# Sums and stores of the down products' left sides moved behind the next pair's weights; residual rows fetched one at a time

## The chip, the cores and the metric

One core of a Trainium2 chip runs the kernel. The metric is device time in microseconds (us) of one execution; lower is better.

## The reference

One transformer-like block on 1024 tokens (and 16 meta tokens) of width 1024. A Mamba-2 branch and a differential-attention branch are merged into `h`; the change touches only what follows, the feed-forward part:

```python
u2 = rmsnorm(h, norm_ffn_g)
h = h + (silu(u2 @ w_gate_ffn) * (u2 @ w_up_ffn)) @ w_down_ffn
out = rmsnorm(h, norm_final_g)
```

`w_gate_ffn` and `w_up_ffn` are 1024 x 2816, `w_down_ffn` is 2816 x 1024, all float32.

## The kernel before

Every float32 product is made of three matmuls of split operands: a side is rounded (`hi`, by ACT's CAST) and the rest kept (`lo`, a subtraction on POOL or DVE, both in `split_to`, L919 and L920). The three feed-forward products are cut by Strassen's scheme: seven half-size products replace eight, and the sides of the products are sums of quarters.

The hidden columns are worked in 11 pairs of 128-row blocks (`pair` 0 to 10). A pair has a gate half and an up half. Each half loads its weights in two parts (`Weights.load`, L948): the first, "kh0", goes into one of two buffers of the tag `raw`; the second, "kh1", into the tag `ht`, whose five buffers hold four tiles of product 7's right side for the whole loop, so that all kh1 parts share one buffer. `Weights.make` builds seven sides from them (L986 on DVE, then the split; sides 3 and 4 are split straight from the loaded tile). `Half.run` makes the seven products in the order 2, 5, 4, 3, 1, 6, 7 (L1000, 12 matmuls each, 168 a pair), and DVE folds them into the tile `gu` (L1015 to L1026). Product 3 starts on its bank when L1017 has read it, product 7 when L1022 has. In the text 2g is product 2 of the gate half, 3u product 3 of the up half.

`up_out` (L1045 to L1048) multiplies silu(gate) by up. `left_sides` then makes the left sides of the down products on DVE (L1058, L1061, L1063, L1064, L1065; L1026 and L1048 must come first for the last three) and stores them to DRAM (`hid_d`): three stores of 256 KB and one of 1 MB (L1067).

The down products run as 77 steps `s` (7 products of 11 steps, 48 matmuls in 4 banks by three, 12 a step). A step loads a left side (`ra`, 256 KB) and one or two quarters of `w_down_ffn` (`rb`, 256 KB each), five steps deep, and splits them on ACT and DVE (`down_make`). Steps 0 to 4 are loaded in the last pair; from step 5 on the pool `dn` is used, which also holds the eight residual rows blocks `hr0` to `hr7` (512 KB each) and `gf` (512 KB). `add_part` adds finished banks to the rows.

All loads and stores go through SP's queue in order. The order of the instructions on each engine is made from the written program by a scheduler that models time, so a moved line can move its neighbours too; each engine then executes in that order.

Of the kernel before, what the change touches and what calls it, by code (L numbers as in the profile page):

```python
# [9 lines left out]
F32 = mybir.dt.float32  # L10
F32R = mybir.dt.float32r
AF = mybir.ActivationFunctionType
ALU = mybir.AluOpType
# [4 lines left out]
P = 128  # L18
D = 1024
# [4 lines left out]
NT = SEQ // P  # L24
# [18 lines left out]
def tile_hybrid_block(  # L43
# [7 lines left out]
    nc = tc.nc  # L51
# [9 lines left out]
    def nm(s):  # L61
        seq[0] += 1
        return f"{s}_{seq[0]}"
# [69 lines left out]
    h_d = dram([SEQ, D], "h_d")  # L133
    hid_d = dram([7, FF // 2, 512], "hid_d")
# [113 lines left out]
    def gates_block(b):  # L248
# [9 lines left out]
        out=gbh, in0=par[:, PR_GB : PR_GB + 16], scalar1=0.5, scalar2=None, op0=ALU.mult  # L258
# [3 lines left out]
        out=g08, in0=par[:, PR_SUB : PR_SUB + 1], scalar1=1.0 - LAM_INIT, scalar2=None,  # L262
# [4 lines left out]
    with tc.tile_pool(name="ssd", bufs=1, reuse_waits="tile") as sp:  # L267
# [4 lines left out]
        def t2(name, tag="t2", bufs=4):  # L272
# [6 lines left out]
            out=tri, in_=tri, pattern=[[1, P]], compare_op=ALU.is_ge, fill=0.0, base=0,  # L279
# [5 lines left out]
            out=sel, in_=sel, pattern=[[0, P]], compare_op=ALU.is_ge, fill=0.0, base=-(P - 1),  # L285
# [7 lines left out]
            out=cbh, in0=par[:, PR_CB : PR_CB + 12], scalar1=0.5, scalar2=None, op0=ALU.mult  # L293
# [19 lines left out]
            out=wd[:, :, 2 * H : 3 * H], in0=wdr, in1=wd[:, :, 0:H].bitcast(F32), op=ALU.subtract  # L313
# [4 lines left out]
            out=fold, in0=ident[: 4 * H, 0:H], in1=ident[: 4 * H, 2 * H : 3 * H], op=ALU.add  # L318
# [89 lines left out]
        for b in (8, 9, 10, 11, 0, 1, 2, 3, 4, 5, 6, 7):  # L408
            if b == 0:
# [10 lines left out]
                out=hh[:, :L], in0=raw[:, 0:L], scalar1=cwh[:, b, 0:1], scalar2=cbh[:, b : b + 1],  # L420
                op0=ALU.mult, op1=ALU.add,
            )
            for k in range(1, 4):
                nc.vector.scalar_tensor_tensor(
                    out=hh[:, :L], in0=raw[:, k : k + L], scalar=cwh[:, b, k : k + 1],
                    in1=hh[:, :L], op0=ALU.mult, op1=ALU.add,
# [6 lines left out]
            else:  # L433
                act = cT[:, b - 10, :]
            nc.vector.scalar_tensor_tensor(
                out=act, in0=raw[:, :L], scalar=1.0, in1=hh[:, :L], op0=ALU.add, op1=ALU.mult
# [19 lines left out]
        for c in range(NC):  # L456
# [8 lines left out]
            for g in range(2):  # L465
# [4 lines left out]
                if last:  # L470
# [3 lines left out]
                    out=v8(xds[:R]), in0=v8(xdt[:R]), in1=bc(dst, g), op=ALU.mult  # L474
# [8 lines left out]
                else:  # L483
                    nc.gpsimd.tensor_tensor(
                        out=v8(snew), in0=v8(prev[g]), in1=bc(cdk, g), op=ALU.mult
# [6 lines left out]
            for g in range(2):  # L492
# [7 lines left out]
                out=cbm, in0=pcb[:, : 2 * P].rearrange("p (g l) -> p g l", g=2),  # L500
                in1=tri.unsqueeze(1).to_broadcast([P, 2, P]), op=ALU.mult,
            )
            y = t4("y")
            for g in range(2):
# [7 lines left out]
                for hq in range(2):  # L512
# [3 lines left out]
                    for j in range(4):  # L516
                        nc.vector.tensor_scalar(
                            out=m3[:, j, :], in0=b3[:, hq * 4 + j, :],
# [5 lines left out]
                        out=m3, in0=m3, in1=cbm[:, g, :].unsqueeze(1).to_broadcast([P, 4, P]),  # L524
                        op=ALU.mult,
# [13 lines left out]
                    out=v8(xD), in0=v8(xs[:, c, gs]),  # L539
                    in1=dsk[:, g * 8 : g * 8 + 8].unsqueeze(2).to_broadcast([P, 8, HD]),  # L540
                    op=ALU.mult,
# [11 lines left out]
    with tc.tile_pool(name="att", bufs=1, reuse_waits="tile") as ap:  # L553
# [6 lines left out]
            out=base, in_=base, pattern=[[-1, L]], compare_op=ALU.is_ge, fill=-1e30,  # L560
# [3 lines left out]
        for i, a in enumerate((lambda_q1, lambda_q2, lambda_k1, lambda_k2)):  # L564
# [7 lines left out]
            out=lam[:, 2:3], in0=lam[:, 1:2], in1=lam[:, 0:1], op=ALU.subtract  # L572
# [3 lines left out]
            out=nlam, in0=lam[:, 2:3], scalar1=-LAM_INIT, scalar2=None, op0=ALU.add  # L576
# [5 lines left out]
        for t in vms + ams:  # L582
            nc.vector.tensor_scalar(
                out=t, in0=base[:, : t.shape[1]], scalar1=0.0, scalar2=None, op0=ALU.mult
# [3 lines left out]
        for i in range(2):  # L588
            for c in range(2):
                z = slice(64 - 64 * c, 128 - 64 * c)  # L590
                nc.gpsimd.tensor_scalar(
                    out=kls[i][c][z], in0=base[z], scalar1=0.0, scalar2=None, op0=ALU.mult
# [7 lines left out]
        for h in range(AH):  # L600
# [21 lines left out]
            def evac_k(ps, o, w):  # L622
# [22 lines left out]
                out=vm[64 : 64 + NM], in0=ptm[:NM, :P], in1=vm[:NM].bitcast(F32),  # L645
                op=ALU.subtract,
            )
            for q in range(2):
                pt = ps_mm()
                for j in range(4):  # L650
# [6 lines left out]
                    out=vl[:, sl4, :], in0=p3, in1=vh[:, sl4, :].bitcast(F32), op=ALU.subtract  # L657
# [6 lines left out]
            for pr2 in range(NT // 2):  # L664
                arows = []
                for i in (2 * pr2, 2 * pr2 + 1):
# [9 lines left out]
                    for comp, (qt, kt) in enumerate(((q0, k0), (q1, k1))):  # L676
                        S = ap.tile([P, L], F32, tag="S", name=nm("S"), bufs=6)
                        sts.append(S)
                        for n, (o, w) in enumerate(pieces):
# [10 lines left out]
                                out=S[:, o : o + w], in0=ps[:, :w],  # L690
                                in1=base[:, L - W + o : L - W + o + w], scale=1.0,
# [5 lines left out]
                            out=nmx, in0=mx[:, col : col + 1], scalar1=-slope, scalar2=None,  # L697
# [11 lines left out]
                        out=rho, in0=sm[:, 0:1], scalar=nlam, in1=sm[:, 3:4], op0=ALU.mult,  # L709
# [195 lines left out]
    fp = ffn_pool.__enter__()  # L905
# [30 lines left out]
    class Weights:  # L936


        def __init__(self, w, pair):
            self.w, self.pair, self.m, self.two_ = w, pair, {}, {}  # L940
            self.load()
# [90 lines left out]
    def gate_banks():  # L1032
        return ps_mm(), ps_mm(), ps_sc(), ps_sc()
# [18 lines left out]

    SLOT = {1: 0, 2: 1, 5: 2, 6: 3, 3: 4, 4: 5, 7: 6}

    def left_sides(G, U, pair):
        rows = slice(pair * P, (pair + 1) * P)
        a11, a12, a21, a22 = G[:, 0, T1], G[:, 1, T1], G[:, 0, T2], G[:, 1, T2]
        vtt(out=U[:, 0, T2], in0=a21, in1=a22, op=ALU.add)  # L1058
        nc.sync.dma_start(hid_d[SLOT[4], rows, :], a22)
        d = fp.tile([P, 512], F32, tag="tmp", name=nm("d"), bufs=3)  # L1060
        vtt(out=d, in0=a12, in1=a22, op=ALU.subtract)  # L1061
        nc.sync.dma_start(hid_d[SLOT[7], rows, :], d)
        vtt(out=U[:, 0, T1], in0=a11, in1=a22, op=ALU.add)  # L1063
        vtt(out=U[:, 1, T1], in0=a11, in1=a12, op=ALU.add)  # L1064
        vtt(out=U[:, 1, T2], in0=a21, in1=a11, op=ALU.subtract)  # L1065
        nc.sync.dma_start(hid_d[SLOT[3], rows, :], a11)
        nc.sync.dma_start(  # L1067
            hid_d[0:4, rows, :].rearrange("s p t -> p s t"),
            U.rearrange("p a (b t) -> p (a b) t", t=512),
        )  # L1070

    def w_out_rows(t, before_last=None):
        hts = []
# [165 lines left out]
    up_w.make(7)  # L1239
    up.run(7)  # L1240
    up_out(G, U, up, 0)
    left_sides(G, U, 0)

    NP = NF // 2
    downs = [(i, f) for i in (1, 5, 4, 7, 3, 2, 6) for f in range(NP)]
# [51 lines left out]
    for pair in range(1, NP):  # L1297
        G, U = new_pair()
        last = pair == NP - 1
        for w in (w_gate_ffn, w_up_ffn):  # L1300
            gate_side = w is w_gate_ffn
            A = Weights(w[0], pair)
            A.make(*order7)
            h = Half(A, G if gate_side else U, (gate_banks if gate_side else up_banks)())
            if last and not gate_side:
                for s, pool in ((0, st), (1, wk)):
                    down_load(s, f512(fp, "tmp", 3), f1k(st, "raw", 2))
                    down_make(s, f512(fp, "tmp", 3), *pair_of(pool))
                h.run(*order7[:5])
                down_load(2, f512(fp, "tmp", 3), f1k(st, "raw", 2))  # L1310
                down_make(2, f512(fp, "tmp", 3), *pair_of(st))
                h.run(*order7[5:])
                for s in (3, 4):
                    down_load(s, f512(st, "gt", 2), f1k(st, "raw", 2))
            else:
                h.run(*order7)
            if gate_side:
                gate_out(G, h)
            else:
                up_out(G, U, h, pair)  # L1320
                left_sides(G, U, pair)

    b4 = gate_banks()
    for s in range(3):
        down_mm(downs, b4, [(s, j) for j in range(4)])
# [4 lines left out]
    with tc.tile_pool(name="dn", bufs=1, side="right", reuse_waits="tile") as dn:  # L1330
# [7 lines left out]
        def dn_load(s):  # L1338
            if s < len(downs) and s > 4:
                down_load(s, f512(dn, "ra", 5), f1k(dn, "rb", 5))  # L1340
# [2 lines left out]
        dn_make(4)  # L1343
        rows = []
        for r in range(NT):
            ht = dn.tile([P, D], F32, name=f"hr{r}")
            nc.sync.dma_start(ht, h_d[r * P : (r + 1) * P, :])
            rows.append(ht)
        gf = dn.tile([P, D], F32, name="gf")
        nc.sync.dma_start(gf, norm_final_g.partition_broadcast(P))  # L1350
        for s in range(5, 9):
            dn_load(s)
        parts = {
            1: ((0, 0, 1), (1, 1, 1)), 2: ((1, 0, 1), (1, 1, -1)), 3: ((0, 1, 1), (1, 1, 1)),
            4: ((0, 0, 1), (1, 0, 1)), 5: ((0, 0, -1), (0, 1, 1)), 6: ((1, 1, 1),),
# [28 lines left out]
        def store(r, n):  # L1384
            nc.sync.dma_start(out2[r * P : (r + 1) * P, N2[n]], jks[r][:, N2[n]])
# [17 lines left out]
        for p in range(7):  # L1403
            i = downs[p * NP][0]
            banks = b4 if p == 0 else (up_banks if p % 2 else gate_banks)()
            for f in range(3 if p == 0 else 0, NP):
                s = p * NP + f
                dn_load(s + 4)
                if s + 2 < len(downs) and s + 2 > 4:
                    dn_make(s + 2)  # L1410
                if p < 6 or f < NP - 2:
                    down_mm(downs, banks, [(s, j) for j in range(4)])
                elif f == NP - 1:
                    down_mm(downs, banks, [(q, j) for j in range(4) for q in (s - 1, s)])
                for _ in range(2 if i in (2, 6) else 1):
                    if later:
                        later.pop(0)()
            for t, n, sign in parts[i]:
                for j in range(4):
                    if p < 6:  # L1420
                        later.append(
                            lambda a=(i, banks[j], j, t, n, sign): add_part(*a)
                        )
            if i == 3:
                later += [lambda r=r: first_rows(r) for r in range(4)]
            if i == 2:
                for j in range(4):
                    later.append(lambda r=4 + j: (square(r, 0), gain(r, 0, nc.gpsimd)))
# [62 lines left out]
```

## Time and profile before

| what | value |
|---|---|
| median of 3 runs | 2026.34 us (2026.12 to 2028.18) |
| the profiled execution | 2029.1 us |
| its span, first to last instruction | 2026.7 us |
| matmuls on TensorE (PE) busy | 1923.2 us, 95% of the span |
| VectorE (DVE) busy | 1252.8 us, 62% |
| GpSimd (POOL) busy | 567.1 us, 28% |
| DMA moved | 241.38 MB |

PE's busy time counts overlapping matmuls, so 95% is not the share of its peak. What counts is when PE sits idle and at which of its two clock levels it runs.

### The profile page before, as it was taken

The numbers are of one execution on the slowest core, as the hardware profiler recorded it, in microseconds if no ns is written. First come the engines' busy times: TensorE is split into PE (matmuls) and PEld (weight loads), VectorE is DVE, ScalarE is ACT, GpSimd is POOL, SyncE is SP. The second block draws the span as 40 slices with busy tenths as digits, with TensorE's granted clock in tenths as the row PEclk, the third lists the DMA queues.
The fourth block names the chain that finished last, engine by engine and source line by source line (L and its number), as shares of the span: only waits on it lengthen the run. The fifth ranks groups of instructions, "written<-read, shape, count | busy, mean of one in ns | idle before, by whom it ended". The sixth has DMA issues, their size and how long they took to land.

```text
span 2026.7 us, 27727 instructions
## 1 busy us (share of the span) xinstructions
PE 1923.2 (95%) x10478; PEld 1668.0 (82%) x10478; DVE 1252.8 (62%) x2387; ACT 762.1 (38%) x1443; POOL 567.1 (28%) x363
## 2 busy tenths in 40 slices
PE   7999999999999999999999999889999998969998
PEld 7999777789999999888978899767777776758886
DVE  5656678555766566654663443585566656648887
ACT  5333222245555455553331124532222222224454
POOL 2223444411111111110122244344444544400002
PEclk9999999999999999999999999999999999989999
DMA  5111344311111211123765444322322232368865
GB/s 174 49 33 53 97 140 133 112 45 50 53 45 46 61 51 40 51 68 121 253 226 173 151 156 160 111 89 84 93 78 92 80 113 85 114 250 304 313 218 198
DMA packets 185935, 241.38 MB, mean 119 GB/s; under 512 B 13517, under 2 KB 128442, under 8 KB 185802
## 3 DMA queue, kind: packets, MB, share of 16 engines
q1 hardware_dynamic: 185658, 239.09, 36.7%
q8 instruction: 82, 1.34, 0.3%
q10 hardware_dynamic: 144, 0.52, 0.1%
q14 instruction: 51, 0.42, 0.1%
HBM read 181.48 MB, written 53.84 MB: 116 GB/s over the span
## 4 chain that ended last, share of the span: by engine, by line
PE 77%; DVE 13%; DMA 6%; issue 1%; ACT 1%; POOL 0%; SPq 0%; DVEq 0%; POOLq 0%; ACTq 0%
PE mm L108 14%; PE mm L109 14%; PE mm L110 14%; PE sc L1000 5%; PE tp L1000 4%; DVE sm L986 3%; DMA raw<-in_w_up_ffn_dram 3%; PE mm L1000 3%; PE sc L109 2%; PE sc L108 2%; PE sc L110 2%; PE tp L729 2%; PE sc L681 1%; PE sc L684 1%; PE sc L529 1%
## 5 line engine op out<-in xcount | busy, mean ns | idle before, releaser
L89 POOL TENSOR_TENSOR wlo<-raw,whi 128x1024 fp32r<-128x1024 f32 x68 | 176.4, 2594 | 685.8 <-ACT whi L87 614.3
L108 PE MATMUL mm<-uTh,whi 128*128 128x346 f32 (+2 forms) x1008 | 360.4, 358 | 7.5 <-DVE kl L626 2.4
L109 PE MATMUL mm<-uTh,wlo 128*128 128x346 f32 (+2 forms) x1008 | 359.5, 357 | 0.0
L110 PE MATMUL mm<-uTl,whi 128*128 128x346 f32 (+2 forms) x1008 | 358.8, 356 | 0.0
L108 PEld LDWEIGHTS mm<-uTh,whi 128*128 128x128 f32 x1008 | 190.9, 189 | 28.5 <-issue 8.4
L110 PEld LDWEIGHTS mm<-uTl,whi 128*128 128x128 f32 x1008 | 191.0, 189 | 18.7 <-issue 3.9
L109 PEld LDWEIGHTS mm<-uTh,wlo 128*128 128x128 f32 x1008 | 190.9, 189 | 17.7 <-issue 3.4
L920 POOL TENSOR_TENSOR wlo<-sm,whi 128x512 fp32r<-128x512 f32 x88 | 129.7, 1493 | 161.9 <-ACT whi L919 161.9
L919 ACT CAST whi<-sm 128x512 fp32r<-128x512 f32 x88 | 52.7, 619 | 215.4 <-DVE sm L986 95.8
L700 ACT ACTIVATE S<-S,mx 128x272 f32<-128x272 f32 (+7 forms) x128 | 101.0, 791 | 54.7 <-DVE mx L696 53.1
L986 DVE TENSOR_TENSOR sm<-raw,raw 128x512 f32<-128x512 f32 x66 | 54.6, 864 | 67.8 <-DMA raw<-in_w_up_ffn_dram 64.5
L920 POOL TENSOR_TENSOR lo<-raw,hi 128x512 fp32r<-128x512 f32 x44 | 65.5, 1488 | 88.8 <-ACT hi L919 88.8
L87 ACT CAST whi<-raw 128x1024 fp32r<-128x1024 f32 x68 | 71.2, 1047 | 50.6 <-PE mm L110 41.9
L748 DVE TENSOR_TENSOR atl<-tp,ath 128x512 fp32r<-128x512 f32 (+1 forms) x80 | 50.5, 634 | 61.8 <-ACT ath L747 61.5
L986 DVE TENSOR_TENSOR sm<-raw 128x512 f32<-128x512 f32 x44 | 50.6, 1154 | 58.7 <-DMA raw<-in_w_gate_ffn_dram 37.7
L1000 PE MATMUL mm<-t2a,hi 128*128 128x512 f32 x176 | 65.8, 433 | 21.8 <-DVE gu L1017 17.7
L919 ACT CAST dhi<-ra 128x512 fp32r<-128x512 f32 x72 | 44.7, 621 | 109.8 <-issue 53.6
L689 DVE CUSTOM_DVE_ANT_0 S<-sc,base 128x272 f32<-128x272 f32 (+7 forms) x128 | 62.0, 493 | 28.2 <-PE sc L684 27.0
L681 PE MATMUL sc<-k,q 128*128 128x144 f32 (+6 forms) x224 | 76.7, 349 | 1.7 <-ACT S L700 1.1
L689 DVE CUSTOM_DVE_ANT_0 S<-sc,base,mx 128x348 f32<-128x348 f32 (+4 forms) x96 | 56.1, 585 | 34.6 <-PE sc L684 31.2
L108 PE MATMUL mm<-whi,uTh 128*128 128x256 f32 x256 | 73.9, 290 | 3.5 <-ACT whi L100 3.3
L109 PE MATMUL mm<-whi,uTl 128*128 128x256 f32 x256 | 74.8, 293 | 0.1
(398 smaller groups left out, 5200.7 us busy)
## 6 DMA issues: line engine op xcount, KB each, us to landing
raw<-in_w_in_dram SPq DMA_DIRECT2D x60, 512.0 KB, 4.0
rb<-in_w_down_ffn_dram SPq DMA_DIRECT2D x82, 256.0 KB, 5.4
ra<-hid_d SPq DMA_DIRECT2D x74, 256.0 KB, 4.6
raw<-in_w_gate_ffn_dram SPq DMA_DIRECT2D x24, 512.0 KB
raw<-in_w_up_ffn_dram SPq DMA_DIRECT2D x24, 512.0 KB, 5.8
hid_d<-gu SPq DMA_DIRECT2D x11, 1024.0 KB, 5.1
rb<-in_w_down_ffn_dram SPq DMA_DIRECT2D x22, 512.0 KB, 6.3
bcs<-acs_d SPq DMA_DIRECT2D x16, 512.0 KB, 5.0
```

Of the source, the lines that this page charges most:

```text
L87: nc.scalar.copy(hi, raw)
L89: nc.gpsimd.tensor_tensor(out=lo, in0=raw, in1=hi.bitcast(F32), op=ALU.subtract)
L108: nc.tensor.matmul(ps, lh, rh, start=first, stop=False)
L109: nc.tensor.matmul(ps, ll, rh, start=False, stop=False)
L110: nc.tensor.matmul(ps, lh, rl, start=False, stop=last)
L681: nc.tensor.matmul(ps[:, :w], qt[:, qs], kt[:, o : o + w], start=True, stop=False)
L689: nc.vector.tensor_tensor_reduce(out=S[:, o : o + w], in0=ps[:, :w], in1=base[:, L - W + o : L - W + o + w], scale=1.0, scalar=-3e38 if n ...
L700: nc.scalar.activation(S[:, :W], S[:, :W], AF.Exp, scale=slope, bias=nmx, accum_out=sm[:, comp : comp + 1],)
L919: nc.scalar.copy(hi, src)
L920: eng.tensor_tensor(out=lo, in0=src, in1=hi.bitcast(F32), op=ALU.subtract)
L986: vtt(out=tmp, in0=a, in1=b, op=op)
L1000: nc.tensor.matmul(ps, a[:, ki, :], b, start=first and ki == 0 and n == 0, stop=ki == KH - 1 and n == 2, skip_group_check=True,)
```

## The change

`left_sides` becomes a class with two methods. `sums()` makes the same five DVE operations, now written behind the next pair's gate `make`. `store()` issues the same four stores, now written behind the load of the next pair's up weights. After the last pair both follow at once, as before. In the down products the rows and `gf` are no longer fetched ahead of the loads of steps 5 to 8: one row follows the loads at steps 5, 7, 9 and one at each step from 11 on, `gf` comes at step 33. And `dn_load(s + 4)` is called only for `s > 4`; before, it was also called at steps 3 and 4, which loaded steps 7 and 8 a second time.

```diff
-    def left_sides(G, U, pair):
...
+    class LeftSides:
...
+        def sums(self):
+            G, U = self.G, self.U
...
+            self.d = fp.tile([P, 512], F32, tag="tmp", name=nm("d"), bufs=3)
+            vtt(out=U[:, 0, T2], in0=a21, in1=a22, op=ALU.add)
+            vtt(out=self.d, in0=a12, in1=a22, op=ALU.subtract)
+            vtt(out=U[:, 0, T1], in0=a11, in1=a22, op=ALU.add)
+            vtt(out=U[:, 1, T1], in0=a11, in1=a12, op=ALU.add)
+            vtt(out=U[:, 1, T2], in0=a21, in1=a11, op=ALU.subtract)
+
+        def store(self):
+            G, U, rows = self.G, self.U, self.rows
+            nc.sync.dma_start(hid_d[SLOT[7], rows, :], self.d)
+            nc.sync.dma_start(hid_d[SLOT[3], rows, :], G[:, 0, T1])
+            nc.sync.dma_start(hid_d[SLOT[4], rows, :], G[:, 1, T2])
+            nc.sync.dma_start(
+                hid_d[0:4, rows, :].rearrange("s p t -> p s t"),
+                U.rearrange("p a (b t) -> p (a b) t", t=512),
+            )
...
             A = Weights(w[0], pair)
+            if not gate_side:
+                before.store()
             A.make(*order7)
+            if gate_side:
+                before.sums()
...
                 up_out(G, U, h, pair)
-                left_sides(G, U, pair)
-
+                before = LeftSides(G, U, pair)
+
+    before.sums()
+    before.store()
...
-            ht = dn.tile([P, D], F32, name=f"hr{r}")
-            nc.sync.dma_start(ht, h_d[r * P : (r + 1) * P, :])
-            rows.append(ht)
+            rows.append(dn.tile([P, D], F32, name=f"hr{r}"))
         gf = dn.tile([P, D], F32, name="gf")
-        nc.sync.dma_start(gf, norm_final_g.partition_broadcast(P))
         for s in range(5, 9):
             dn_load(s)
+        fetch = [(rows[r], h_d[r * P : (r + 1) * P, :]) for r in range(NT)]
...
-                dn_load(s + 4)
+                if s > 4:
+                    dn_load(s + 4)
+                if s in (5, 7, 9) or s >= NP and fetch:
+                    nc.sync.dma_start(*fetch.pop(0))
+                if s == 3 * NP:
+                    nc.sync.dma_start(gf, norm_final_g.partition_broadcast(P))
```

New line numbers: the sums are L1065 to L1069, the 1 MB store L1076, the other stores L1073 to L1075, the down loads L1259 and L1271, the rows L1424, `gf` L1426.

**SP's queue in the pair loop.** One pair's stretch in the middle of the loop. Of the `raw` loads the first of two from the same tensor is kh0, the second kh1. Before:

```order
L1059 DMA hid_d<-gu_14196 128x512
L1062 DMA hid_d<-d_14473 128x512
L1066 DMA hid_d<-gu_14196 128x512
L1067 DMA hid_d<-gu_14196 128x4x512
L948 DMA raw_14621<-in_w_up_ffn_dram 128x4x256
L948 DMA raw_14767<-in_w_gate_ffn_dram 128x4x256
L948 DMA raw_14769<-in_w_gate_ffn_dram 128x4x256
L948 DMA raw_14904<-in_w_up_ffn_dram 128x4x256
```

Now:

```order
L948 DMA raw_14900<-in_w_up_ffn_dram 128x4x256
L948 DMA raw_14902<-in_w_up_ffn_dram 128x4x256
L1075 DMA hid_d<-gu_14471 128x512
L1073 DMA hid_d<-d_14795 128x512
L1074 DMA hid_d<-gu_14471 128x512
L1076 DMA hid_d<-gu_14471 128x4x512
L948 DMA raw_15042<-in_w_gate_ffn_dram 128x4x256
L948 DMA raw_15044<-in_w_gate_ffn_dram 128x4x256
```

The up kh1 load stood behind the 1 MB store and now stands ahead of all four; the gate kh0 load of the pair after stands behind the 1 MB store. In three of the pairs (every third) that gate load stands two rows higher, ahead of the last two stores.

**DVE in the pair loop**, from the last folds of one pair (`gu_14481`, now `gu_14471`) on; `sm` are the sums of weights. Before:

```order
L1047 TENSOR_TENSOR gu_14481<-gu_14481 128x512
L1058 TENSOR_TENSOR gu_14481<-gu_14481 128x512
L1061 TENSOR_TENSOR d_14758<-gu_14481 128x512
L986 TENSOR_TENSOR sm_14773<-raw_14767,raw_14769 128x512
L986 TENSOR_TENSOR sm_14779<-raw_14767,raw_14769 128x512
L1026 TENSOR_TENSOR gu_14481<-tp_14659,gu_14481 128x512
L1048 TENSOR_TENSOR gu_14481<-gu_14481 128x512
L986 TENSOR_TENSOR sm_14791<-raw_14767,raw_14769 128x512
L1063 TENSOR_TENSOR gu_14481<-gu_14481 128x512
L1064 TENSOR_TENSOR gu_14481<-gu_14481 128x512
L1065 TENSOR_TENSOR gu_14481<-gu_14481 128x512
L986 TENSOR_TENSOR sm_14910<-raw_14904,raw_14906 128x512
```

Now:

```order
L1066 TENSOR_TENSOR d_14795<-gu_14471 128x512
L986 TENSOR_TENSOR sm_14910<-raw_14900,raw_14902 128x512
L986 TENSOR_TENSOR sm_14916<-raw_14900,raw_14902 128x512
L1026 TENSOR_TENSOR gu_14471<-tp_14659,gu_14471 128x512
L986 TENSOR_TENSOR sm_14928<-raw_14900,raw_14902 128x512
L1048 TENSOR_TENSOR gu_14471<-gu_14471 128x512
L1067 TENSOR_TENSOR gu_14471<-gu_14471 128x512
L1068 TENSOR_TENSOR gu_14471<-gu_14471 128x512
L1069 TENSOR_TENSOR gu_14471<-gu_14471 128x512
L1017 TENSOR_TENSOR gu_14756<-mm_14802,gu_14756 128x512
L1019 TENSOR_TENSOR gu_14756<-mm_14801,gu_14756 128x512
L986 TENSOR_TENSOR sm_15072<-raw_15042 128x512
```

The sums of the gate's weights are gone from here (they are made ahead of the folds of the up half), the sums of the up weights (`sm_14910` on) stand ahead of the three left-side sums, and L1017 of the next gate behind these; in two of three pairs L1017 stands higher, ahead of these three sums. The last row reads the gate kh0 load that follows the 1 MB store.

**SP's queue from the last pair to the down products.** Before:

```order
L1067 DMA hid_d<-gu_15336 128x4x512
L1347 DMA hr_15733<-h_d 128x1024
L1347 DMA hr_15735<-h_d 128x1024
L1347 DMA hr_15737<-h_d 128x1024
L1347 DMA hr_15739<-h_d 128x1024
L1347 DMA hr_15741<-h_d 128x1024
L1347 DMA hr_15743<-h_d 128x1024
L1347 DMA hr_15745<-h_d 128x1024
L1347 DMA hr_15747<-h_d 128x1024
L1350 DMA gf<-in_norm_final_g_dram 128x1024
L1250 DMA ra_15751<-hid_d 128x512
```

Now:

```order
L1076 DMA hid_d<-gu_15326 128x4x512
L1259 DMA ra_15742<-hid_d 128x512
L1271 DMA rb_15743<-in_w_down_ffn_dram 128x512 x2
L1259 DMA ra_15747<-hid_d 128x512
L1271 DMA rb_15748<-in_w_down_ffn_dram 128x512 x2
L1259 DMA ra_15752<-hid_d 128x512
L1271 DMA rb_15753<-in_w_down_ffn_dram 128x512 x2
L1259 DMA ra_15757<-hid_d 128x512
L1271 DMA rb_15758<-in_w_down_ffn_dram 128x512 x2
L1259 DMA ra_15802<-hid_d 128x512
L1271 DMA rb_15803<-in_w_down_ffn_dram 128x512 x2
L1424 DMA hr_15733<-h_d 128x1024
```

Nine transfers of 512 KB stood between the store and step 5's loads; now the loads of steps 5 to 9 follow the store, and the first row comes behind them.

## Rows read from the trace of the kernel before

**Rows 1.** Waits of PE, 1400 to 1790 us: us in total, times, longest.

```profile
PE mm L1000 <- DVE gu L1017: 17.7, 9, 2.3
PE tp L1000 <- DVE gu L1022: 6.3, 8, 0.8
PE av L1000 <- ACT whi L919: 5.7, 8, 0.7
```

**Rows 2.** Timeline of PE: start, duration, [idle before, and what ended it].

```profile
1612.74 0.49 PE L1000 MATMUL av<-t2b,whi 128*128 128x512 f32 x1 [0.71 <-ACT whi L919]
...
1632.40 0.50 PE L1000 MATMUL mm<-t2a,hi 128*128 128x512 f32 x1 [1.92 <-DVE gu L1017]
...
1652.60 0.50 PE L1000 MATMUL tp<-b,whi 128*128 128x512 f32 x1 [0.78 <-DVE gu L1022]
...
1656.35 0.50 PE L1000 MATMUL av<-t2b,whi 128*128 128x512 f32 x1 [0.71 <-ACT whi L919]
```

**Rows 3.** Timeline of DVE, the same pair.

```profile
1619.64 1.78 DVE L1065 TENSOR_TENSOR gu<-gu 128x512 f32<-128x512 f32 x1
1628.16 1.90 DVE L986 TENSOR_TENSOR sm<-raw,raw 128x512 f32<-128x512 f32 x3 [6.74 <-DMA raw<-in_w_up_ffn_dram]
...
1631.66 0.68 DVE L1017 TENSOR_TENSOR gu<-mm,gu 128x512 f32<-128x512 f32 x1
...
1647.16 0.86 DVE L986 TENSOR_TENSOR sm<-raw 128x512 f32<-128x512 f32 x1 [2.24 <-DMA raw<-in_w_up_ffn_dram]
```

**Rows 4.** Timeline of SP's queue, the same pair.

```profile
1621.44 0.37 SPq L1067 DMA_DIRECT2D hid_d<-gu  x1
1621.91 0.46 SPq L948 DMA_DIRECT2D raw<-in_w_up_ffn_dram  x1
...
1643.33 0.37 SPq L948 DMA_DIRECT2D raw<-in_w_up_ffn_dram  x1
```

**Rows 5.** Timeline of ACT and POOL, the same pair.

```profile
1613.64 0.61 ACT L919 CAST hi<-raw 128x512 fp32r<-128x512 f32 x1
...
1617.42 1.74 POOL L920 TENSOR_TENSOR lo<-raw,hi 128x512 fp32r<-128x512 f32 x1
```

**Rows 6.** The chain of waits: start, us, what it was.

```profile
1434.12 1.21 DVE sm L986 x2
...
1463.83 5.54 PE sc L1000 x24
...
1744.56 1.20 DVE sm L986 x2
```

**Rows 7.** Timeline of DVE behind the last pair.

```profile
1794.21 0.69 DVE L1063 TENSOR_TENSOR gu<-gu 128x512 f32<-128x512 f32 x1
```

**Rows 8.** Timeline of SP's queue behind the last pair.

```profile
1796.13 0.37 SPq L1067 DMA_DIRECT2D hid_d<-gu  x1
1796.61 5.39 SPq L1347 DMA_DIRECT2D hr<-h_d  x8
...
1805.46 0.32 SPq L1250 DMA_DIRECT2D ra<-hid_d  x1
```

**Rows 9.** Timeline of ACT and PE, step 5.

```profile
1815.13 0.62 ACT L919 CAST dhi<-ra 128x512 fp32r<-128x512 f32 x1 [17.17 <-DMA ra<-hid_d]
...
1818.36 0.80 PE L108 MATMUL mm<-dhi 128*128 128x512 f32 x1 [15.19 <-ACT dhi L919]
```

**Rows 10.** Windows: busy us (instructions) of PE, PEld, DVE, ACT, POOL; PEclk, DMA share, GB/s.

```profile
1498.00:1503.00 5.00, 4.58 (x13) 3.62 (x14) 2.59 (x3) 1.53 (x3) 3.83 (x3) 0.66 0.02 3
...
1815.00:1826.00 11.00, 7.64 (x24) 6.06 (x24) 5.39 (x9) 3.72 (x7) 0.00 (x0) 0.64 1.04 381
1826.00:1836.00 10.00, 9.81 (x44) 7.91 (x43) 9.10 (x15) 6.47 (x12) 0.00 (x0) 1.00 1.04 386
```

**Rows 11.** The page's DMA issues: count, KB each, median us to landing.

```profile
ra<-hid_d SPq DMA_DIRECT2D x74, 256.0 KB, 4.6
hid_d<-gu SPq DMA_DIRECT2D x11, 1024.0 KB, 5.1
```

More of the change, by code (lines that the diff above doesn't have):

```diff
@@ L1053, in tile_hybrid_block, with __init__ @@
     SLOT = {1: 0, 2: 1, 5: 2, 6: 3, 3: 4, 4: 5, 7: 6}
-    def left_sides(G, U, pair):
[L1056 to L1070, printed above, removed]
+    class LeftSides:
+        def __init__(self, G, U, pair):
+            self.G, self.U, self.rows = G, U, slice(pair * P, (pair + 1) * P)
+        def sums(self):
+            G, U = self.G, self.U
+            a11, a12, a21, a22 = G[:, 0, T1], G[:, 1, T1], G[:, 0, T2], G[:, 1, T2]
+            self.d = fp.tile([P, 512], F32, tag="tmp", name=nm("d"), bufs=3)
[13 more added lines that the diff above has]
+            )
     def w_out_rows(t, before_last=None):
@@ L1241, in tile_hybrid_block @@
     up_out(G, U, up, 0)
-    left_sides(G, U, 0)
+    before = LeftSides(G, U, 0)
     NP = NF // 2
```

## Prediction

> **What bounds the kernel now.** PE. I read the waits of PE over the pair loop first: what holds it there are three things, once a pair each [rows 1]. The timeline of PE shows them in one pair: 0.71 us for a cast, 1.92 for L1017, 0.78 for L1022 [rows 2]. The next pair's first product starts 43.61 us after this one's (1612.74 to 1656.35). Undisturbed, 24 matmuls take 5.54 us [rows 6], 0.231 each, so 168 take 38.8. With the three waits that is 42.2. Of the 1.4 that remain I put half to the two matmuls behind the first, which wait for casts as well, and leave half with PE as gaps that stay (my choice; no row parts them). So a pair without waits would take about 39.5 us.
>
> Over seven pairs the mean is (1744.56 - 1434.12) / 7 = 44.35 us [rows 6], 0.74 more than the pair above. Behind some L1017 waits PE runs at the lower level: 13 matmuls in 4.58 us at a granted clock of 0.66, a mixture of 1.2 and 2.4 GHz [rows 10], against 3.0 at 0.231. That costs 1.6 us in about every second pair.
>
> Why does L1017 come late? On DVE it stands behind sums of the up weights, and these wait 6.74 us for their load [rows 3]. SP issues that load at 1621.91, right behind the 1 MB store of 1621.44 [rows 4], and that store waits for L1065, which ends at 1621.42 [rows 3]. The load's buffer was free when POOL ended its last `lo` at 1619.16 [rows 5]. So the store holds the load, and the load, which also queues its bytes behind the store, holds DVE and then PE.
>
> Behind the loop there is one large hole: PE waits 15.19 us for step 5 [rows 9]. Its first load is issued at 1805.46, nine transfers behind the store of 1796.13 [rows 8]. PE then needs 7.64 us for 24 matmuls at a clock of 0.64 [rows 10].
>
> **The change part by part.**
>
> *The up load.* Nothing is added to an engine: five DVE operations and four stores a pair stay. The load no longer waits for the sums. From below it comes 2.75 us earlier (1619.16 for 1621.91). More is likely, since the cast ahead of that `lo` also moves: its buffer comes free when 3u of the pair before is done. Call that moment T. Cast 0.61, `lo` 1.74 [rows 5], issue: T + 2.5. A load that stands alone lands after 3.8 us (issued 1643.33, used 1647.16) [rows 3, 4], where behind the store it took 6.25. So it lands at T + 6.3.
>
> *The sums.* Behind T PE still has about 40 matmuls (rest of 1u, 6u, 2g, 7u), to T + 9.2. DVE has by then made two or three sums of weights (1.9 us for three [rows 3]). L1026 takes 7u's result, one more sum of weights and L1048 follow; by T + 13 the three left-side sums can start. Beside POOL one takes 1.78 us, 1.70 from start to start [rows 3], alone 0.69 [rows 7]. POOL splits the up weights at that time, so I take 5.2 for three: to T + 18.2.
>
> The Trainium skill ("SBUF — State Buffer", "Who interferes with whom") states that a DVE instruction with two SBUF inputs contends with a GpSimd one that reads SBUF. By that rule the sums pay this price wherever POOL has work; rows 3 against 7 agree. Without it they would take 2.0, and the wait below would go: that is the floor rival's case.
>
> *Which wait is next.* In the order shown in the section on the change, L1017 follows the sums: done at T + 19. PE wants 3g after 5g, 4g, 1g and a few of 6g: 40 + 40 matmuls, T + 18.5, so it waits 0.5, or up to 2 if the store of `d`, on whose buffer a sum of weights waits, lands late. In the two other orders L1017 is early and L1022 is the late one. There the gate kh0 load goes out behind the 1 MB store at T + 18.7 and lands 6.25 later, T + 25; a sum of weights that reads it, L1020 and L1022 (0.7 to 1 each) end at T + 27.5 to 28. PE wants 7g at T + 27 to 28.5. I take a wait of 1.5 us a pair, bounds 0 and 4. What was late is thus mostly cured, and what is late next is the sums themselves or the load behind their store. The cast's wait of 0.71 and its two followers go, since the casts of the next gate no longer stand behind one that waits for 7u.
>
> *Sum for a pair:* 39.5 + 1.5 + 0.3 for slow clock, which I let remain in one pair of five, is 41.3. Against 44.35 that is 3.05, over nine pairs 27 us. (The first and the last pair have their own orders; I count them together as one of the nine.)
>
> *The down loads.* The 1 MB store lands 5.1 us after its issue [rows 11], at 1801.2; the left side of step 5 follows it directly, 0.26 MB at 381 GB/s [rows 10] or 0.7 us: 1801.9. Before, PE started 3.2 us after the cast of that tile (1815.13 to 1818.36 [rows 9]), so now at 1805.1 for 1818.36: 13.3 us. Bounds: 11.5 if the two `rb` wait for other bytes, 15.4 if the slow clock goes too (7.64 less 24 times 0.231 is 2.1). I take 13.
>
> *The rows.* They are hidden by PE's steps, 12 matmuls or 2.8 us each, if the queue can carry them. A step of the first product loads 0.79 MB, with half a row 1.05; one of the second 0.52, with a row 1.05. At 386 GB/s [rows 10] that takes 2.7 us: it just fits, and the loads of five steps are ahead of the first row. If it didn't fit, all nine transfers (4.7 MB, 12 us) would at worst come back as waits; half of that is a rival. Also gone are two steps' loads that were fetched twice (74 `ra` loads [rows 11], where 72 are needed), 1.6 MB or 4 us of queue in the same stretch.
>
> *Total:* 27 + 13 = 40 us. The profiled execution took 2029.1 (span 2026.7); 1989 by it. It lies 2.8 above the median of the runs shown, 2026.34, so **1986**.
>
> **The rivals.**
>
> *Floor.* The sums fall into a pause of POOL, or DVE gets its loads early enough; no wait is left and the clock stays up. A pair takes 39.5: 44 us, and 15 behind the loop: 1967. For it: PE ran from 1826 to 1836 at a clock of 1.00 where nothing held it [rows 10]. Against it: sums and POOL's `lo` meet today [rows 3, 5], and the splits of the up weights now fall on the same stretch.
>
> *New waits as long as the old.* DVE is held by the gate kh0 load behind the store of the sums, so L1020 and L1022 come as late as L1017 does now. A pair takes 43.6, seven tenths less: about 6 us, with 13: 2007. For it: the load takes 6.25 behind such a store today [rows 4], and everything on DVE stands in line. Against: PE needs L1022 some nine microseconds later than L1017.
>
> *The clock.* The short waits that remain are each followed by a stretch as in rows 10: 1.6 us a pair, 42.6 in all, 16 us instead of 27: 1997. The skill ("TensorE: Matmul & The Clock Gate", "A second HAM failure mode") describes such frequent short idles that bring the clock down again and again. Here it went down behind waits of about 2 us and not behind each.
>
> *The rows collide.* The down loads come late in steps 9 to 20; 6 of the 13 us are given back: 1992.
>
> *Slower.* The new wait on DVE outgrows the gain. It decides where a pair takes more than 44.35 + 13 / 9 = 45.8, that is a new wait of 6 us. With the gate kh0 load landing at T + 31 (twice its 6.25) and a slow stretch behind each wait (1.6) it would be 47: 9 times 2.65 less 13 is 11 us more, 2037. Against: nothing in rows 4 shows a load of 512 KB that slow.
>
> That the order didn't change as written is excluded by the rows in the section on the change.
>
> **How the numbers follow.** Forecast (1980 to 1990) 0.45, clock 0.13, rows collide 0.10, floor 0.12, new waits 0.16, slower 0.03, none 0.01. From 1967 to 2009 about 0.82 is held: the floor is just inside, of the new waits most. A change under 0.2% (4 us) can't be told from none. Faster 0.95, same 0.02, slower 0.03.
>
> **What would show it.** Right: in the pair loop the up load's wait on DVE (6.74) is gone or short, the load is issued ahead of the 1 MB store, pairs follow at about 41.3 us, and the PE wait on L1017 shrinks below 2 or becomes one on L1022; step 5 starts some 2 us behind step 4 and the three sums still take 1.7 us each beside POOL. Wrong: pairs at 43 us or more with DVE waiting for a gate load; PE waits on ACT's `dhi` after step 5; or a mean clock below 1.00 through the loop.

## The result

The changed kernel takes 1966.74 us (median of 4, 1965.29 to 1969.95); before, measured beside it, 2026.42 (2026.12 to 2028.18). The ratio is 0.9706, 95% interval 0.9689 to 0.9723: 59.7 us faster, where 40 were forecast; 1966.7 lies just below the range. The profiled execution took 1969.95, its span went from 2026.7 to 1968.2, 58.5 less.

The head of the page after: the span, the engines' busy time, the granted clock in 40 slices, the bytes.

```profile
span 1968.2 us, 27717 instructions
...
PE 1904.9 (97%) x10478; PEld 1662.5 (84%) x10478; DVE 1241.7 (63%) x2387; ACT 761.7 (39%) x1443; POOL 563.4 (29%) x363
...
PEclk9999999999999999999999999999999999999999
...
DMA packets 185071, 239.80 MB, mean 122 GB/s; under 512 B 13421, under 2 KB 128346, under 8 KB 184938
```

The work is the same, less the 1.6 MB that were loaded twice; PE is busy 18 us less with the same 10478 matmuls. That is the first hint that the time lost was more than the waits. In the slices, 9 stands for 0.9 and more.

Waits of PE in six pairs after, where rows 1 had three names once in each pair:

```profile
PE mm L1000 <- POOL lo L920: 3.7, 3, 1.3
PE mm L1000 <- DVE gu L1017: 1.7, 2, 1.4
PE tp L1000 <- POOL lo L920: 0.5, 2, 0.2
PE sc L1000 <- ACT gu L1015: 0.2, 1, 0.2
```

The PE timeline shows a cycle of three pairs: a wait for `lo` (1480.16, 1600.16 and 1719.07 below), one for L1017 (1.84 at 1398.31, 1.42 at 1518.90, 0.24 at 1637.73), and little else.

```profile
1480.16 0.50 PE L1000 MATMUL mm<-t2a,lo 128*128 128x512 f32 x1 [1.23 <-POOL lo L920]
1518.90 0.47 PE L1000 MATMUL mm<-t2a,hi 128*128 128x512 f32 x1 [1.42 <-DVE gu L1017]
1600.16 0.50 PE L1000 MATMUL mm<-t2a,lo 128*128 128x512 f32 x1 [1.26 <-POOL lo L920]
1719.07 0.51 PE L1000 MATMUL mm<-t2a,lo 128*128 128x512 f32 x1 [1.26 <-POOL lo L920]
```

Six pairs take 1719.07 - 1480.16 = 238.91 us, 39.82 each, where rows 6 give 44.35. Windows over whole pairs part this into busy and idle time of PE (columns as in rows 10). First seven pairs before, then six after:

```profile
1434.12:1744.56 310.44, 285.96 (x1178) 222.78 (x1176) 187.13 (x218) 81.28 (x140) 148.53 (x98) 0.98 0.28 89
```

```profile
1480.16:1719.07 238.91, 233.88 (x1009) 188.89 (x1009) 154.28 (x186) 69.49 (x121) 123.57 (x85) 1.00 0.32 102
```

For a pair: busy 40.85 before and 38.98 after, idle 3.50 and 0.84. So 2.66 us of waits are gone and 1.87 us of busy time with them.

One pair after, on SP, DVE and PE; it answers to rows 3 and 4.

```profile
1537.90 8.10 SPq L948 DMA_DIRECT2D raw<-in_w_up_ffn_dram  x2
...
1560.59 0.37 SPq L1076 DMA_DIRECT2D hid_d<-gu  x1
```

```profile
1549.50 2.31 DVE L986 TENSOR_TENSOR sm<-raw,raw 128x512 f32<-128x512 f32 x2 [1.28 <-DMA raw<-in_w_up_ffn_dram]
...
1552.35 0.68 DVE L1017 TENSOR_TENSOR gu<-mm,gu 128x512 f32<-128x512 f32 x1
...
1557.08 1.78 DVE L1068 TENSOR_TENSOR gu<-gu 128x512 f32<-128x512 f32 x1
1558.78 1.78 DVE L1069 TENSOR_TENSOR gu<-gu 128x512 f32<-128x512 f32 x1
```

```profile
1555.58 0.39 PE L1000 MATMUL mm<-t2a,hi 128*128 128x512 f32 x1
```

Both up loads are out by 1546, 14 us ahead of the 1 MB store; DVE waits 1.28 for the second part, which it waited 6.74 for, L1017 ends at 1553.0, and PE takes up its product (1555.58) 2.5 us later without a wait. DVE still waits 5.58 for the first part (up to 1541.73), but no wait of PE follows from that here. The sums still take up to 1.78.

Behind the loop, answering to rows 8 and 9:

```profile
1750.32 0.37 SPq L1076 DMA_DIRECT2D hid_d<-gu  x1
1750.79 0.44 SPq L1259 DMA_DIRECT2D ra<-hid_d  x1
```

```profile
1760.95 0.50 PE L108 MATMUL mm<-dhi 128*128 128x512 f32 x1 [2.94 <-ACT dhi L919]
```

Step 5's load follows the store directly, and its wait is 2.94 instead of 15.19. The span then parts like this: the wait for step 5 begins 45.2 us earlier (1818.36 - 15.19 against 1760.95 - 2.94), it is 12.2 shorter, and what follows it takes 207.3 for 208.3. 45.2 + 12.2 + 1.1 is 58.5. Nine times 4.53 (44.35 - 39.82) is 40.8 of the 45.2. Nine is the count of the prediction, which took the first and the last pair together as one; the other 4.4 is what one pair more gives. The two at the ends give about 11 together. From 1278 on, where both kernels stand at the same matmul, 422 matmuls take 113.5 us before, into the last products of the first pair, and some 106.5 after; the last 228 ahead of the wait for step 5 take 57.6 before, and 226 of them 53.2 after. The first gives the most, since a wait stands there that only before has:

```profile
1347.90 0.79 PE L1000 MATMUL mm<-t1b,whi 128*128 128x512 f32 x1 [4.27 <-ACT whi L919]
```

### The profile page after: what moved, and what is told of

It reads as the page before. It is cut to its first block, busy times and chain, and to the rows that moved or that the text cites. A ratio compares the mean times of both kernels' runs of the same rounds, so it can differ in the third digit from the quotient of the medians.

```text
span 1968.2 us, 27717 instructions
## 1 busy us (share of the span) xinstructions
PE 1904.9 (97%) x10478; PEld 1662.5 (84%) x10478; DVE 1241.7 (63%) x2387; ACT 761.7 (39%) x1443; POOL 563.4 (29%) x363
## 4 chain that ended last, share of the span: by engine, by line
PE 74%; DVE 11%; DMA 6%; POOL 3%; issue 3%; ACT 2%; SPq 0%; POOLq 0%; DVEq 0%; ACTq 0%
PE mm L108 15%; PE mm L109 15%; PE mm L110 15%; PE sc L1000 3%; PE tp L1000 3%; PE sc L109 2%; PE sc L108 2%; PE sc L110 2%; DVE sm L986 2%; PE tp L729 2%; POOL wlo L920 2%; PE sc L529 1%; PE sc L681 1%; PE sc L684 1%; DMA raw<-in_w_gate_ffn_dram 1%
## 5 line engine op out<-in xcount | busy, mean ns | idle before, releaser
L920 POOL TENSOR_TENSOR wlo<-sm,whi 128x512 fp32r<-128x512 f32 x88 | 134.5, 1552 | 124.8 <-ACT whi L919 124.8
L110 PE MATMUL mm<-wlo,uTh 128*128 128x256 f32 x256 | 73.9, 290 | 1.1 <-DVE wlo L102 1.1
L684 PE MATMUL sc<-kl,q 128*128 128x144 f32 (+6 forms) x224 | 72.2, 325 | 0.0
```

What stands on the lines that cost most here:

```text
L110: nc.tensor.matmul(ps, lh, rl, start=False, stop=last)
L684: nc.tensor.matmul(ps[:, :w], qt[:, qs], kl[comp][:, o : o + w], start=False, stop=True,)
L920: eng.tensor_tensor(out=lo, in0=src, in1=hi.bitcast(F32), op=ALU.subtract)
```

## The experiments

Ratios are to the kernel before on the same chip, with 95% intervals.

| kernel | median us | ratio | span |
|---|---|---|---|
| loop alone | 1981.08 | 0.9763 (0.9748 to 0.9778) | 1979.5 |
| rows alone | 2015.24 | 0.9928 (0.9912 to 0.9945) | 2013.5 |
| before, 1 MB store on ScalarE's queue | 2006.40 | 0.9889 (0.9874 to 0.9903) | 2004.7 |
| stores late, sums in the old place | 2016.10 | 0.9942 (0.9924 to 0.9960) | 2011.2 |
| two more sums | 1969.52 | 0.9710 (0.9696 to 0.9725) | 1967.5 |
| rows at once | 1976.99 | 0.9740 (0.9723 to 0.9756) | 1974.0 |
| two steps loaded twice | 1969.70 | 0.9703 (0.9688 to 0.9717) | 1968.8 |

**Which half gave what.** The first kernel has the new loop with the old fetch, the second the old loop with the new fetch.

```diff
-            rows.append(dn.tile([P, D], F32, name=f"hr{r}"))
+            ht = dn.tile([P, D], F32, name=f"hr{r}")
+            nc.sync.dma_start(ht, h_d[r * P : (r + 1) * P, :])
+            rows.append(ht)
         gf = dn.tile([P, D], F32, name="gf")
+        nc.sync.dma_start(gf, norm_final_g.partition_broadcast(P))
...
-                if s > 4:
-                    dn_load(s + 4)
-                if s in (5, 7, 9) or s >= NP and fetch:
-                    nc.sync.dma_start(*fetch.pop(0))
...
+                dn_load(s + 4)
```

> The new place of the sums and stores in the pair loop alone; the rows of h and the final gain are fetched as before, all nine ahead of the down loads, with the two steps loaded twice. Theory A (the loop gives 45 us as the trace of the changed kernel parts it: the wait for step 5 starts 45.2 us earlier): 1981, and the wait for step 5 is 15 us as before. Rival B (my prediction's split, 27 from the loop and 13 behind it, the surplus of 20 from both together): 1999. Rival C (the surplus came from the rows, which no longer stand in the loop's way): 2005 or more. Pairs follow at 39.8 us under A, 41.3 under B.

> The single fetch of the rows alone, with the loop of before. Theory A (the two halves add, 13 to 14 us are the rows'): 2012 to 2013, the wait for step 5 about 3 us, pairs at 44.35 as before. Rival C (the rows give more than the loop left over): 2000 or less. If the halves need each other (the last pair's late up load holds step 5 as well): 2018 or more.

Theory A holds for both. The rows alone come out at 2011.8 by their ratio. The loop alone is 47.2 us shorter in span, the rows alone 13.2; together 60.4, where the whole change gives 58.5, and spans of one kernel differ by up to 5.5 (1975.8 to 1981.3 for the loop alone). Neither half needs the other. In the loop-alone kernel the old wait at step 5 is back, in the rows-alone kernel the old waits of the loop; the waits of PE from 1340 on, of each:

```profile
PE mm L108 <- ACT dhi L919: 15.0, 2, 14.5
PE mm L1000 <- DVE gu L1017: 3.2, 4, 1.4
```

```profile
PE mm L1000 <- DVE gu L1017: 17.5, 9, 2.3
PE tp L1000 <- DVE gu L1022: 8.2, 9, 2.0
...
PE mm L108 <- ACT dhi L919: 5.3, 2, 3.5
```

**Was it the queue?** Before's order on PE and DVE stays; only the 1 MB store is issued from another engine.

```diff
-        nc.sync.dma_start(
+        nc.scalar.dma_start(
             hid_d[0:4, rows, :].rearrange("s p t -> p s t"),
```

> The kernel before, with its 1 MB store of the sums issued by ScalarE's DMA queue and not by SyncE's; the orders on TensorE and VectorE are those of before. Theory T1 (in SyncE's queue the store held the up load, and by that L1017 and TensorE): the load goes out some 2.7 us earlier, DVE's wait for it falls from 6.7 to about 4, the wait on L1017 (1.97 us a pair) goes, with what follows it (a slower first matmul, a lower clock): 2.5 to 3 us a pair, 23 to 27 in all, about 2001. Rival T2 (the place of the sums on VectorE ahead of the up side's is what costs, whatever the queue): no more than 5 us, 2021 or more. Rival T3 (the store's bytes, beside the load, slow it as much as the queue did): no change, 2026.

T1 holds, with 22 us by span where it had 23 to 27, and a wait of DVE that falls further than its "about 4". One pair on SP and on DVE:

```profile
1605.68 0.38 SPq L948 DMA_DIRECT2D raw<-in_w_up_ffn_dram  x1
```

```profile
1606.13 1.78 DVE L1065 TENSOR_TENSOR gu<-gu 128x512 f32<-128x512 f32 x1
1609.32 1.29 DVE L986 TENSOR_TENSOR sm<-raw,raw 128x512 f32<-128x512 f32 x2 [1.42 <-DMA raw<-in_w_up_ffn_dram]
```

The load goes out before the last sum even starts and is used 3.64 us later, with the store's bytes beside it; DVE waits 1.42 for it. PE no longer waits for L1017 at all; its two other waits in a pair stay. Seven pairs by windows, and these two waits in one of them:

```profile
1429.61:1719.88 290.27, 279.57 (x1177) 220.06 (x1177) 187.09 (x218) 81.32 (x140) 147.06 (x98) 1.00 0.29 96
```

```profile
1471.08 0.50 PE L1000 MATMUL tp<-b,whi 128*128 128x512 f32 x1 [0.78 <-DVE gu L1022]
...
1474.82 0.51 PE L1000 MATMUL av<-t2b,whi 128*128 128x512 f32 x1 [0.71 <-ACT whi L919]
1475.34 0.50 PE L1000 MATMUL mm<-t1b,whi 128*128 128x512 f32 x1
1475.87 0.49 PE L1000 MATMUL mm<-t2a,hi 128*128 128x512 f32 x1
1476.20 0.50 PE L1000 MATMUL av<-t2b,wlo 128*128 128x512 f32 x1
```

A pair takes 41.47, busy 39.94, idle 1.53. So one wait of 1.97 us (rows 1: 17.7 over nine) cost 2.88 (44.35 - 41.47), 0.91 of it in PE's busy time. Most of this surcharge is the clock: 0.98 over the seven pairs before, 1.00 here. It isn't spread over the waits. Behind three of the nine waits for L1017 before (1498.42, 1587.21, 1676.55) the 12 matmuls of 3g take 4.3 to 4.5 us, behind the six others 2.9, where 12 times 0.231 is 2.8. The waits and these three stretches come to 17.7 + 3 x 1.6 = 22.5; the span is 22.0 shorter. Two windows before (columns as in rows 10), around a wait of 1.87 (to 1587.21) and one of 1.92 (to 1632.40):

```profile
1585.00:1590.00 5.00, 3.13 (x9) 2.23 (x8) 4.37 (x4) 2.26 (x4) 5.00 (x4) 0.75 0.00 0
...
1632.00:1637.00 5.00, 4.60 (x20) 3.80 (x21) 4.02 (x6) 2.74 (x5) 4.60 (x4) 1.00 0.01 3
```

The wait for the cast, which stays here, has a surcharge of another kind. In a stream a matmul starts 0.23 us behind the one before; behind this wait the next ones start 0.52, 0.53 and 0.33 apart, 0.7 us in all, at a clock of 1.00.

The Trainium skill ("DMA: Bandwidth & Descriptors", "Issuing engines are not separate DMA queues") says that a second issuing engine saves only the time to initiate a transfer, usually small. Here the measurement shows more: SP's issue of the load stood behind one that waited for a sum, and freeing it was worth 22 us.

**Sums or stores?** The sums go back to the old place; the stores stay behind the up load in the program.

```diff
-            if gate_side:
-                before.sums()
...
                 before = LeftSides(G, U, pair)
-
-    before.sums()
+                before.sums()
```

> The changed kernel with the five sums written in their old place, at the end of a pair, and only the stores written behind the next up load. The orders on SyncE and TensorE are then those of the kernel with the rows alone, row for row, since what sets the order lets a store go when its sums are ready. Theory (the place of the sums is all of the loop's change): 2013 to 2016, pairs at 44.35. Rival (the place of the stores does the work): 1985 or less.

As the theory said, at 2016.10: pairs at 44.41 ((1739.06 - 1472.60) / 6, between the waits for L1022), and the store ahead of the load again:

```profile
1618.91 0.37 SPq L1076 DMA_DIRECT2D hid_d<-gu  x1
1619.37 0.46 SPq L948 DMA_DIRECT2D raw<-in_w_up_ffn_dram  x1
```

So the stores' new place in the program does nothing by itself: without the sums' move the store goes out ahead of the load as before. The reverse, the sums late and the stores written directly behind them, was not run.

**Is DVE just in time?** Two sums a pair are made twice.

```diff
             vtt(out=U[:, 1, T2], in0=a21, in1=a11, op=ALU.subtract)
+            vtt(out=U[:, 0, T1], in0=a11, in1=a22, op=ALU.add)
+            vtt(out=U[:, 1, T1], in0=a11, in1=a12, op=ALU.add)
```

> The changed kernel with two of the five sums made twice (the same results written again): 3.4 us more of VectorE a pair at the 1.7 that one takes beside GpSimd. My prediction left 1.5 us of wait a pair since DVE would be just late for L1017 or L1022. If DVE has no slack there: 3.4 a pair and more, 31 us in all, 1998 or above. If DVE has slack of some microseconds in most pairs, as the few waits of the changed kernel say (L1017 late in one pair of three): 0 to 5 us, 1967 to 1972.

No change: 0.9710 for 0.9706. They took 1.35 and 0.95 us, 2.3 a pair and not 3.4. PE is busy 293.38 of the 300 us from 1440 to 1740 with them, 293.19 without. Waits for L1022 do appear, and those for `lo` shrink; PE's waits from 1340 on:

```profile
PE sc L1000 <- DVE gu L1022: 3.2, 4, 1.1
...
PE mm L1000 <- POOL lo L920: 1.3, 1, 1.3
```

So DVE is close to late, as the prediction walked it, but two microseconds more of it are still covered.

**One by one?** All rows at once, behind the loads of steps 5 to 8.

```diff
-        fetch = [(rows[r], h_d[r * P : (r + 1) * P, :]) for r in range(NT)]
+        for r in range(NT):
+            nc.sync.dma_start(rows[r], h_d[r * P : (r + 1) * P, :])
+        nc.sync.dma_start(gf, norm_final_g.partition_broadcast(P))
...
```

> The changed kernel with all eight rows of h and the final gain fetched at once, behind the loads of steps 5 to 8 and ahead of step 9's, and not one by one. Theory A (what counts is that the first down loads no longer stand behind the nine fetches; the fetches, 4.7 MB or 12 us of queue, are then mostly covered by steps 3 to 8 of TensorE): the wait for step 5 stays near 3 us, one wait of 2 to 4 us before step 9 or 10: 1969 to 1972. Rival B (only the spreading hides them): all 12 us come back as a wait at step 9, with a slow stretch behind it: 1979 to 1983.

Between the two. Step 5 waits 2.92 as in the changed kernel, and a new wait stands before step 9:

```profile
1777.70 0.79 PE L108 MATMUL mm<-dhi 128*128 128x512 f32 x1 [5.78 <-ACT dhi L919]
```

This wait is twice A's and half of B's. The ratio is 0.0034 or 7 us over the changed kernel's, though the two intervals just touch. So of the 13 us behind the loop about half comes from the order alone, the rest from the spreading.

**The double loads.** `if s > 4:` is dropped, so steps 7 and 8 are loaded twice.

> The changed kernel with the loads of steps 7 and 8 made twice again, 1.57 MB or 4 us of queue where the queue is full (share 1.03 from 1770 to 1800). Theory A (the steps already loaded cover it): 1966 to 1968. Rival B (the queue has no room there): TensorE waits 3 to 4 us more between steps 7 and 12, 1970 to 1971.

A holds, by the trace and by the ratio, 0.9703 for 0.9706 (the median alone, 1969.70, would not tell A from B). A single wait of 0.90 us appears at 1790, where B had 3 to 4. By the trace the 1.6 MB were worth no more than that; the ratio alone can't tell anything under 3 us.

**A further step?** In the changed kernel the 1 MB store, of every pair or of the last alone, moved to ScalarE's queue.

> The changed kernel with its 1 MB store on ScalarE's DMA queue; the order on TensorE is that of the changed kernel, but for one place. Theory A (in the loop no load that TensorE waits for stands behind the store any more; only the last pair's store still holds step 5's loads): pairs stay at 39.8, the wait of 2.9 us for step 5 goes: 1963 to 1965. Rival B (the gate load behind the store still costs something, as my prediction's remaining wait of 1.5 us had it): pairs fall to 39.2 or less, 1958 to 1960. Rival C (ScalarE, which must now wait for the sums, holds casts): 1970 or more.

> The changed kernel once more, beside the next two on one chip: ratio 0.9706 as before, bounds 0.969 to 0.972.

> The changed kernel with every pair's 1 MB store on ScalarE's queue, once more. If the 7 us by which its profiled span was shorter (1961.2 against 1968.2) are its own: pairs at 39.35, the wait for step 5 below 2 us, 0.3 per cent below the changed kernel beside it, ratio 0.967. If they came from the chip's spread: within 0.1 per cent of the changed kernel.

> The changed kernel with only the last pair's 1 MB store on ScalarE's queue; all other orders are those of the changed kernel. Theory A (the wait of 2.9 us for step 5 is the loads standing behind this store): it falls to 1 or below, 2 to 4 us less than the changed kernel. Rival B (the loads wait for the store's bytes, whichever queue sends them): no change.

The first run seemed a gain: span 1961.2, ratio 0.9687 (0.9672 to 0.9701). Repeated beside the changed kernel it is none: 0.9705 (0.9688 to 0.9723) for every pair, 0.9708 (0.9691 to 0.9725) for the last, 0.9701 (0.9684 to 0.9718) for the changed kernel itself. The 7 us were spread. For the last pair rival B is nearer, by another way than written. Step 5 is in time, but SP stops at the loads of the third step behind the loop, and PE waits for later steps instead. The waits of SP's queue and PE's timeline in the kernel with the last store moved:

```profile
SPq L1271 <- DMA hid_d<-gu: 7.5, 1, 7.5
```

```profile
1757.34 0.73 PE L110 MATMUL mm<-dlo,dhi 128*128 128x512 f32 x2 [1.58 <-DVE dlo L920]
1762.78 0.50 PE L108 MATMUL mm<-dhi 128*128 128x512 f32 x1 [1.52 <-ACT dhi L919]
```

By the trace SP waits 7.5 us for the store to land, though another engine issued it; with every pair's store moved it is 7.7 and, repeated, 7.4. Why this load waits for that store, the runs don't show.

## Why the prediction fell short

The direction and the two mechanisms that it named were right; the loop was mis-sized, 27 us forecast and 45 measured. By the terms of the sum for a pair:

| term | forecast | measured | over nine pairs |
|---|---|---|---|
| a pair without waits | 39.5 | 38.98 | 4.7 |
| waits that remain | 1.5 | 0.84 | 5.9 |
| slow clock that remains | 0.3 | 0 | 2.7 |
| first and last pair | together one of the nine | two, 4.4 more | 4.4 |

These are 17.7 of the 18 us. The remaining-wait term failed most: 1.5 us a pair forecast, 0.84 measured.

- *The up load.* Right, and shown: with the queue alone freed L1017 is in time.
- *The sums.* Right in size, up to 1.78 beside GpSimd after as before. The rule of the Trainium skill that the prediction cites ("SBUF — State Buffer", "Who interferes with whom") agrees. But no PE wait hangs on them in two of three pairs, and two more of them cost nothing.
- *Which wait is next.* Here the step failed, in its last line. L1017 behind the sums was late as forecast (1.84, 1.42 and 0.24 for "0.5, or up to 2"), but that order stands in one pair of three. The gate load does stand behind the 1 MB store (1518.18 and 1518.65 on SP), DVE waits 6.93 us for it, and L1022 ends where the text had it, just when PE wants its product: 0.4 us ahead in this pair (rows below), 0.3 and 1.4 in the next two. The text's own times, T + 27.5 to 28 against T + 27 to 28.5, said as much; 1.5 was taken all the same, for every pair. A wait that it did not name, for `lo`, is 1.2 in one pair of three. DVE, then PE:

```profile
1526.48 0.69 DVE L986 TENSOR_TENSOR sm<-raw 128x512 f32<-128x512 f32 x1 [6.93 <-DMA raw<-in_w_gate_ffn_dram]
...
1527.81 0.69 DVE L1022 TENSOR_TENSOR gu<-sc,gu 128x512 f32<-128x512 f32 x1
```

```profile
1528.90 0.39 PE L1000 MATMUL sc<-b,whi 128*128 128x512 f32 x1
```

- *The wait for 7u* (L1022 in rows 1) went, as the sum assumed without a reason. The traces show the reason in PE's order: before, 7u stands directly behind 1u, whose sum it needs; after, 1u's last matmul starts at 1537.15 and 7u's first at 1549.83, with other products between. L1022 ends 4.4 us ahead of it (DVE, then PE):

```profile
1544.77 0.68 DVE L1022 TENSOR_TENSOR gu<-tp,gu 128x512 f32<-128x512 f32 x1
```

```profile
1537.15 0.39 PE L1000 MATMUL tp<-t2b,whi 128*128 128x512 f32 x1
...
1549.83 0.39 PE L1000 MATMUL tp<-b,whi 128*128 128x512 f32 x1
```

- *Gaps that stay.* Half of 1.4 us was left with PE by choice. Nearly all of it went: with the waits their slow first matmuls go, 168 matmuls take 38.98, 0.232 each, for the 38.8 of the undisturbed stream.
- *The clock.* Granted 1.00 through the loop; 0.3 was left. In rows 10 a wait of 1.96, which ends at 1498.42, is followed by 0.66; after, the 5 us behind the 1.42 of 1518.90 are at 1.00.
- *The first and the last pair.* Counted together as one of the nine, 3.05 us; they gave about 11, the last as much as a pair of the middle, the first more. The first had a wait of 4.27 of its own that went too. It was in the trace and was not looked at apart.
- *The down loads.* 13 forecast; 12.2 of wait and 1.1 behind it measured, 13.2 by the rows alone.
- *The rows.* Hidden, as forecast: after step 5 PE waits for no load, with the queue at a share of 1.03 from 1780 to 1800.

Of the rivals the floor came true, at 1967 for 1966.7, though not by its reason: a pair still has waits, 39.82 for its 39.5, and the two pairs at the ends, counted as one there too, made up the difference. That it agrees to 1 us is luck.

What stays open: of the 47 us that the loop gives alone, the queue gives 22 when it is freed alone. The other 25 come only with the sums' move. The trace shows with them a new order on PE, in which the waits for L1022 and for the cast are gone; no run changes that order by itself, and which of the steps that set it moved 7u isn't known.

## What to carry to other kernels

A queue that waits in order is part of the path: look at what stands behind each store that waits for a result, and try the store on another queue before moving any arithmetic. Price a wait of TensorE by the pair with and without it, not by its length: here 1.97 us of wait cost 2.88, most of the surplus in three slow stretches among nine waits. When a change moves one engine's work under a scheduler, compare the order of the bound engine too, and go through the first and the last turn of the loop apart.

## What was not expected of the hardware

- The granted clock stayed at 1.00 with one or two waits of 1.2 to 1.8 us in each three pairs, and with two of 0.7 to 0.8 in each pair. In the kernel before, rows 10 show 0.66, between 1.2 and 2.4 GHz, behind a wait of 1.96, but behind others of 1.88 to 1.96 it stayed at 1.00; so the length of a wait alone doesn't tell. The Trainium skill ("TensorE: Matmul & The Clock Gate", "A second HAM failure mode") warns of frequent short idles; these runs show some that cost the clock and some that don't.
- A load of 512 KB took 3.64 us with a 1 MB store issued by another engine 2 us behind it, 6.25 behind the same store in one queue [rows 3, 4].
- By the trace a store from ScalarE's queue held SP's queue for 7.4 to 7.7 us, in three traces, until it had landed.
